# Moving the start addresses of three large SBUF tiles and of the pools after them

## The chip, the core and the metric

The kernel runs on one core of a Trainium2 chip. The metric is the device time of one execution in microseconds, lower is better; the time before is 2186.32 us, the median of three runs (2185.72 to 2187.77). The engines that matter are TensorE (PE in the profile; its weight loads are listed separately as PEld), VectorE (DVE), ScalarE (ACT), GpSimd (POOL) and SyncE (SP), whose queue issues most of the transfers. The on-chip memory (SBUF) has 128 partitions; a tile occupies the same byte range in every partition, and "address" below means the byte offset of a tile's start within a partition.

## What is computed

A two-layer decoder trunk on a sequence of 1024 tokens with 1024 features, all in float32:

```python
for layer in range(DEPTH):              # DEPTH = 2
    if layer < N_A_LAYERS:              # layer 0: HGRN2 gated linear recurrence, 8 heads of 128
        mix = hgrn2_mixer(h, hgrn_w_in[layer], lower_bounds[layer], hgrn_gnorm_w[layer], hgrn_w_out[layer])
    else:                               # layer 1: sliding-window attention, 16 query and 4 key/value heads
        mix = swa_sink_mixer(h, k_shared, v_shared, swa_w_q[j], swa_sinks[j], bias, mask, swa_w_out[j])
    h = layer_norm(ALPHA * h + mix, ln_mix_g[layer], ln_mix_b[layer])
    ff = conv_ffn(h, ffn_w_in[layer], ffn_conv_w[layer], ffn_conv_b[layer], ffn_w_out[layer])
    h = layer_norm(ALPHA * h + ff, ln_ffn_g[layer], ln_ffn_b[layer])

def conv_ffn(h, w_in, conv_w, conv_b, w_out):   # 1024 -> 2 x 2816 -> 1024
    u = causal_depthwise_conv(h @ w_in, conv_w) + conv_b
    a, b = jnp.split(u, 2, axis=-1)
    return (jax.nn.silu(a) * b) @ w_out
```

## The kernel before

**Precision by splitting.** A float32 operand is split into a high part in a reduced float format (`F32R`) and the low rest. `split` (L216) makes the high part with a ScalarE cast (L218) and the low part with a VectorE subtraction (L166). A product is then three matmuls into one PSUM accumulator, made by `mm3` (L190 to L194): high weights by high data (L191), high weights by low data (L192), low weights by high data (L193). Each matmul has a moving operand (the data that stream through the array, 512 or 256 columns of 4 bytes per partition) and a stationary operand (a 128x128 block, 512 bytes per partition), which a weight load puts into the array while the matmul before it runs. In the profile a matmul's name is written `out<-moving,stationary`; where both operands lie in the same tile, only one name stands.

**The large tiles.** All of them live in SBUF:

- `T` holds the transposed activations in both parts, 64 KiB per partition: 2 parts x 8 blocks x 1024 tokens. It is the moving operand of most products and, in token-major products, the stationary one.
- `Y` (32 KiB) is a row buffer: activations, evacuated products, raw weights.
- `HL` (48 KiB) holds weights or activations in two parts, in slots of 8 KiB or pieces of 4 KiB.
- `HT` (12 KiB) belongs to the pool opened for each feed-forward layer and extends `HL`: pieces 12 to 14 of the weights (`weight_load`) and slot 6 of the down projection (`operands`).
- `rx0` to `rx2` (4 KiB each, in the same pool) receive raw weights from DRAM. In the mixers the same addresses hold `raw0` to `raw2`.
- `TX` (48 KiB, class `Up`) holds three derived activation matrices in two parts. In the down projection its place is taken by `R`.

**The stages.** The order on TensorE is: the HGRN2 mixer (0 to 524 us), its output projection with layer norm and transposition (to 590 us), the up projection of the feed-forward (to 925 us), the down projection (to 1140 us), attention (to 1486 us), its output projection (to 1552 us), the second up projection (to 1887 us) and the second down projection (to the end). Both feed-forward matrices are multiplied with a seven-product scheme on 2x2 blocks. In the up projection (class `Up`, `run` and `product`) each of 22 column blocks runs the products in the order 1, 2, 6, 7, 4, 5, 3; each product is four `mm3`, thus 12 matmuls of 512 columns. Products 1, 2, 4 and 5 take their moving operand from `T`, products 6, 7 and 3 from `TX`. Their stationary operands lie in `HL` for odd column blocks, and in `HL` and `HT` for even ones; products 6 and 7 of an even block use `HT`, and so does product 3 of every third block. In the down projection (class `Down`, `operands` and `product`) both operands of a matmul lie in the same slot, in `HL`, `HT` or `T`.

**The order of the work** is written out by hand: nearly everything is issued within manual schedules, and an `Order` object places vector work between matmuls by a table of costs. None of that depends on addresses.

**Where the tiles lie.** A pool hands out addresses in the order in which its tiles are declared, and pools follow each other in the order in which they are opened. The pool `cp` begins at byte 1152. Its first tiles are `T`, `Y` and `HL`, followed by small constants (`ident`, `nhalf`, `par`, `cwt`, `lbt`, `msk`); after it comes the pool `sm` with small statistics, and then the pool of the current stage. The addresses of the built program, in bytes of a partition:

| tile | start | remainder by 512 | remainder by 64 |
|---|---|---|---|
| `T` | 1152 | 128 | 0 |
| `Y` | 66688 | 128 | 0 |
| `HL` | 99456 | 128 | 0 |
| `HT`, `raw0` | 152032 | 480 | 32 |
| `rx0` (`rx1`, `rx2` 4096 and 8192 further) | 164320 | 480 | 32 |
| `TX`, `R` | 176608 | 480 | 32 |
| work tiles of the recurrence (`V`, `G`, `qs`, `kp`, `qp`, `St`, `og` and others) | from 164320 | 480 | 32 |
| attention's `Kh`; `Kl`, `Vt`; `q`, `X` | 164320; 181792, 189984; from 205408 | 480; 32; 96 | 32 |

Of the kernel before, what the change touches and what calls it, by code (L numbers as in the profile page):

```python
# [10 lines left out]
F32 = mybir.dt.float32  # L11
F32R = mybir.dt.float32r
# [4 lines left out]
P = 128  # L17
S = 1024
D = 1024
NB = S // P  # L20
KC = D // P
# [86 lines left out]
def trunk(ctx: ExitStack, tc: tile.TileContext, a: dict, out: bass.AP):  # L108
# [4 lines left out]

    cp = ctx.enter_context(tc.tile_pool(name="cp", bufs=1))
    sm = ctx.enter_context(tc.tile_pool(name="sm", bufs=2))
    mmp = ctx.enter_context(tc.tile_pool(name="mmp", bufs=4, space=PS))
    axp = ctx.enter_context(tc.tile_pool(name="axp", bufs=2, space=PS))
    drp = ctx.enter_context(tc.tile_pool(name="drp", bufs=1, space=bass.MemoryType.DRAM))

    T = cp.tile([P, 2, KC, S], F32R, name="T")  # L120
    Y = cp.tile([P, 8, D], F32, name="Y")
    HL = cp.tile([P, 12, 1024], F32R, name="HL")
    ident = cp.tile([P, P], F32, name="ident")
    nhalf = cp.tile([P, 1], F32, name="nhalf")
    par = cp.tile([P, 17], F32, name="par")
    cwt = cp.tile([P, 2, 4, 2 * NF], F32, name="cwt")
    lbt = cp.tile([P, 2, NH], F32, name="lbt")
    msk = cp.tile([P, 7 * BL + P], U8, name="msk")
    h2d = drp.tile([P, 8, D], F32, name="h2d")
    ynd = drp.tile([P, 8, D], F32, name="ynd")  # L130
    gd = drp.tile([P, NF, S], F32, name="gd")
# [11 lines left out]
    def urgent():  # L143

        return tc.high_priority(offset=300)
# [8 lines left out]
    def hl_at(i):  # L154
        return HL[:, 2 * i:2 * i + 2, :]

# [33 lines left out]
    def mm3(ps, st, mv, start, stop, n=512):  # L190
        nc.tensor.matmul(ps, st(0), mv(0), start=start, stop=False)  # L191
        nc.tensor.matmul(ps, st(0), mv(1), start=False, stop=False)  # L192
        nc.tensor.matmul(ps, st(1), mv(0), start=False, stop=stop)  # L193
        od.t += 3 * n / 2365.0  # L194
# [5 lines left out]
    def tr(ps, src):  # L200
        nc.tensor.transpose(ps, src, ident)  # L201
        od.t += 0.109

    def proj_T(hl, half, ps):
        for kc in range(KC):
            mm3(ps, lambda i: hl[:, i, kc, :], lambda i: T[:, i, kc, half * 512:(half + 1) * 512],
                kc == 0, kc == KC - 1)
            od.tick()

    def proj_tok(us, tp, ps):  # L210
        for i in range(2):
            for kc in range(KC):
                mm3(ps[:, i * 256:(i + 1) * 256], lambda j: T[:, j, kc, (2 * tp + i) * P:(2 * tp + i + 1) * P],
                    lambda j: us[kc // 4][:, j, kc % 4, :], kc == 0, kc == KC - 1, n=256)
                od.tick()

    def split(hi, lo, src, eng=None):
        nc.scalar.copy(hi, src)  # L218
        return low_part(lo, src, hi, eng)
# [8 lines left out]
    def ln_half(tb, i):  # L228

        if tb not in half_stats:  # L230
            half_stats[tb] = sm.tile([P, 2, 6], F32, name="st", bufs=8)
        nc.vector.bn_stats(half_stats[tb][:, i, :], Y[:, tb, i * 512:(i + 1) * 512])

    def ln_stats(tb):
        st = half_stats.pop(tb)
        mv = sm.tile([P, 2], F32, name="mv")
        rs = sm.tile([P, 1], F32, name="rs")
        nc.vector.bn_aggr(mv, st)
        nc.vector.tensor_scalar(rs, mv[:, 1:2], 1.0, LN_EPS, op0=ALU.mult, op1=ALU.add)  # L239
        nc.gpsimd.tensor_tensor(rs, rs, nhalf, op=ALU.pow)  # L240
        return mv, rs

    def ln_affine(tb, rows, dst, n=1):

        y = Y[:, tb, :]
        mv, rs = ln_stats(tb)
# [8 lines left out]
    def turn_block(tb):  # L255

        ps = psax()
        for kc in range(KC):
            tr(ps[:, kc * P:(kc + 1) * P], Y[:, tb, kc * P:(kc + 1) * P])
        ts = slice(tb * P, (tb + 1) * P)  # L260
        split(T[:, 0, :, ts], T[:, 1, :, ts], ps.rearrange("p (k t) -> p k t", k=KC))

# [10 lines left out]
    def Y_to_T(h0, h1, t0, t1, eng=None):  # L273
        ts = slice(t0 * P, t1 * P)
        split(T[:, 0, h0:h1, ts], T[:, 1, h0:h1, ts], Y[:, h0:h1, ts], eng)

# [17 lines left out]
    def out_part(ps, us, tb, kcs, first=0, last=KC - 1):  # L294
        for kc in kcs:
            mm3(ps, lambda j: T[:, j, kc, tb * P:(tb + 1) * P], lambda j: us[kc][:, j, :], kc == first, kc == last)
            od.tick()

    def out_proj(us, begun, rows, resid, ff, ln):
        tasks, late = [], []  # L300
        for tb in range(NB):
            nc.sync.dma_start(Y[:, tb, :], resid(tb))
        for tb, ps in enumerate(begun):
            out_part(ps, us, tb, [KC - 1])
        for dh in range(2):
# [3 lines left out]
            for tb in range(NB):  # L309
# [8 lines left out]
                else:  # L318
                    ps = psmm()
                    out_part(ps, late if dh else us, tb, range(KC))  # L320
                y = Y[:, tb, dh * 512:(dh + 1) * 512]
                with urgent() if dh else nullcontext():
# [18 lines left out]
    def piece(j):  # L341

        t = HL[:, j, :] if j < 12 else tail["R"][:, j - 12, :]
        return t.rearrange("p (h n) -> p h n", h=2)

    class Up:
# [6 lines left out]
        def row_loads(self):  # L353

            l, b = self.l, a["ln_mix_b"]
            self.rows = HL[:, 7, :].bitcast(F32), self.rx[1]
            nc.sync.dma_start(self.rows[0], bass.AP(tensor=gd1.tensor, offset=gd1.offset + l * D, ap=[[0, P], [1, D]]))
            nc.sync.dma_start(self.rows[1], bass.AP(tensor=b.tensor, offset=b.offset + l * D, ap=[[0, P], [1, D]]))

        def ln(self, tb):  # L360
# [6 lines left out]
            with urgent():  # L367
                for q in range(2):
# [4 lines left out]
                    if tb < 4:  # L373
                        split(T[:, 0, ks, ts], T[:, 1, ks, ts], pv)
                        nc.scalar.copy(hf[:, ks], pv)
# [21 lines left out]
        def weight_load(self, fc):  # L397


            whole = lambda j: (HL[:, j, :] if j < 12 else tail["R"][:, j - 12, :])  # L400
            ws = [whole((0 if fc % 2 else 8) + i) for i in range(6)] + [whole((14, 6, 7)[fc % 3])]
# [1077 lines left out]
def build(arrays):  # L1479
    import concourse.bacc as bacc  # L1480

    nc = bacc.Bacc("TRN2", target_bir_lowering=False, num_devices=1, dynamic_dma_scratch_size=1024)
    aps = {n: nc.dram_tensor(f"in_{n}_dram", v.shape, mybir.dt.from_np(v.dtype), kind="ExternalInput").ap()
           for n, v in arrays.items()}
    out = nc.dram_tensor("out_0_dram", (1, S, D), F32, kind="ExternalOutput").ap()
    with tile.TileContext(nc) as tc, tc.manual_schedule(engines={mybir.EngineType.PE}):
        trunk(tc, aps, out)
    return nc
# [10 lines left out]
```

## Time and profile before

| what | value |
|---|---|
| median of three runs | 2186.32 us (2185.72 to 2187.77) |
| span of the profiled execution (first to last instruction) | 2184.9 us |
| difference between that median and that span | 1.4 us |
| TensorE matmuls busy | 2164.9 us, 99% of the span |
| TensorE weight loads busy | 1811.8 us, 83% |
| VectorE busy | 1762.3 us, 81% |
| ScalarE busy | 893.8 us, 41% |
| GpSimd busy | 120.3 us, 6% |
| mean granted TensorE clock | 0.998 |

The profile is one execution on the chip. Its page gives busy times, the clock in 40 slices, the chain of work that ended last and the costliest groups. Three further views of the trace are used: groups of instructions with their shapes kept apart (name, shape, count, union of busy time, mean duration of one in ns, idle time before), windows (in each stretch of time, the busy time of an engine and the number of instructions that it started there), and the timeline (start, duration, engine, line, names). Consecutive matmuls overlap in the array: a 512-column matmul is shown as lasting about 390 ns, while the next one starts about 227 ns after it. The pace of TensorE is therefore the distance from start to start; the mean duration of a group moves with it, but is not it.

### The profile page before, as it was taken

What the parts mean: (1) busy time and instruction counts of PE and PEld (TensorE: products, weight loads), DVE (VectorE), ACT (ScalarE), POOL (GpSimd) and SP (SyncE); (2) the same over time, 40 slices, a digit from 0 to 9 for tenths busy, and PEclk for the clock granted to TensorE, in tenths of its full rate; (3) what the DMA queues carried; (4) which work ended last, traced back from release to release, by engine and by line L of the source; (5) the groups of instructions that cost most, each with busy time, mean ns of one, the idle gap of its engine ahead of it and who ended that gap; (6) DMA issues with size and microseconds to landing.
All of it is one profiled execution on the core that took longest, in us unless ns stands there. A gap on an engine that the chain in (4) does not pass through costs nothing.

```text
span 2184.9 us, 33220 instructions
## 1 busy us (share of the span) xinstructions
PE 2164.9 (99%) x13188; PEld 1811.8 (83%) x13188; DVE 1762.3 (81%) x2388; ACT 893.8 (41%) x1457; POOL 120.3 (6%) x135
## 2 busy tenths in 40 slices
PE   9999999999999999999999999999999999999998
PEld 8888888898878888888888888878888888888887
DVE  3776665667999988888978568969999988878986
ACT  3233333342444444344433256743544444444430
POOL 1000000000100000000001123211000000000001
PEclk9999999999999999999999999999999999999999
DMA  5654533305223222228854411133223222249762
GB/s 197 232 169 161 183 136 101 99 21 175 98 75 106 87 78 81 83 97 263 290 183 155 126 32 28 32 108 115 87 96 96 79 87 77 78 139 325 235 204 94
DMA packets 229844, 279.05 MB, mean 128 GB/s; under 512 B 29960, under 2 KB 158648, under 8 KB 226872
## 3 DMA queue, kind: packets, MB, share of 16 engines
q1 hardware_dynamic: 228736, 276.53, 38.8%
q8 instruction: 104, 1.70, 0.3%
q10 hardware_dynamic: 856, 0.37, 0.1%
q14 instruction: 52, 0.43, 0.1%
q0 software_dynamic: 96, 0.02, 0.0%
HBM read 213.94 MB, written 62.94 MB: 127 GB/s over the span
## 4 chain that ended last, share of the span: by engine, by line
PE 95%; DVE 4%; ACT 1%; issue 1%; DMA 0%; SPq 0%; DVEq 0%; POOL 0%; ACTq 0%; POOLq 0%
PE psmm L191 20%; PE psmm L193 19%; PE psmm L192 19%; PE psax L192 9%; PE psax L193 9%; PE psax L191 9%; PE psax L197 3%; PE psax L201 1%; PE psmm L201 1%; PE psmm L197 1%; PE psax L1290 1%; DVE HL L166 0%; DVE T L166 0%; PE psmm L735 0%; DVE Y L470 0%
## 5 line engine op out<-in xcount | busy, mean ns | idle before, releaser
L191 PE MATMUL psmm<-T,HL 128*128 128x512 f32 x768 | 307.5, 400 | 0.0
L192 PE MATMUL psmm<-T,HL 128*128 128x512 f32 x768 | 300.3, 391 | 0.0
L193 PE MATMUL psmm<-T,HL 128*128 128x512 f32 x768 | 300.2, 391 | 0.0
L470 DVE SCALAR_TENSOR_TENSOR Y<-Y,cwt 128x1023 f32<-128x1023 f32 (+1 forms) x176 | 225.1, 1281 | 42.7 <-ACT Y L468 39.5
L218 ACT CAST HL<-rx 128x1024 fp32r<-128x1024 f32 (+1 forms) x151 | 151.0, 1004 | 199.6 <-PE psmm L192 48.8
L191 PE MATMUL psmm<-HL,T 128*128 128x256 f32 (+1 forms) x656 | 198.4, 302 | 0.0
L193 PE MATMUL psmm<-HL,T 128*128 128x256 f32 (+1 forms) x656 | 194.3, 296 | 1.4 <-DVE T L166 1.4
L192 PE MATMUL psmm<-HL,T 128*128 128x256 f32 (+1 forms) x656 | 194.0, 296 | 0.0
L166 DVE TENSOR_TENSOR HL<-rx,HL 128x1024 fp32r<-128x1024 f32 (+1 forms) x151 | 174.6, 1161 | 13.4 <-ACT HL L218 13.1
L193 PEld LDWEIGHTS psmm<-T,HL 128*128 128x128 f32 x768 | 144.2, 188 | 31.4
L191 PEld LDWEIGHTS psmm<-T,HL 128*128 128x128 f32 x768 | 144.3, 188 | 30.9 <-issue 0.8
L192 PEld LDWEIGHTS psmm<-T,HL 128*128 128x128 f32 x768 | 144.4, 188 | 28.1
L468 ACT ACTIVATE Y<-Y,cwt 128x1024 f32<-128x1024 f32 x88 | 109.0, 1238 | 103.5 <-DVE Y L457 94.4
L192 PE MATMUL psax<-T,HL 128*128 128x512 f32 x352 | 137.7, 391 | 0.0
L191 PE MATMUL psax<-T,HL 128*128 128x512 f32 x352 | 137.7, 391 | 0.0
L193 PE MATMUL psax<-T,HL 128*128 128x512 f32 x352 | 137.4, 390 | 0.0
L191 PEld LDWEIGHTS psmm<-HL,T 128*128 128x128 f32 x656 | 125.2, 191 | 6.6 <-issue 2.9
L193 PEld LDWEIGHTS psmm<-HL,T 128*128 128x128 f32 x656 | 125.2, 191 | 5.2 <-DVE T L166 2.0
L192 PEld LDWEIGHTS psmm<-HL,T 128*128 128x128 f32 x656 | 125.4, 191 | 3.3
L240 POOL TENSOR_TENSOR rs<-rs,nhalf 128x1 f32<-128x1 f32 x32 | 45.6, 1425 | 1415.4 <-DVE rs L239 1415.4
L166 DVE TENSOR_TENSOR HL<-raw,HL 128x1024 fp32r<-128x1024 f32 x51 | 62.4, 1226 | 66.9 <-ACT HL L173 66.6
L218 ACT CAST HT<-rx 128x1024 fp32r<-128x1024 f32 (+1 forms) x37 | 35.5, 959 | 114.3 <-DVE rx L424 75.1
(293 smaller groups left out, 5113.0 us busy)
## 6 DMA issues: line engine op xcount, KB each, us to landing
rx<-in_ffn_w_in_dram SPq DMA_DIRECT2D x136, 256.0 KB, 3.4
rx<-gd SPq DMA_DIRECT2D x118, 256.0 KB, 3.6
Y<-in_ffn_w_out_dram SPq DMA_DIRECT2D x44, 512.0 KB, 5.7
bsd<-Y SPq DMA_DIRECT2D x22, 1024.0 KB, 4.5
gd<-Y SPq DMA_DIRECT2D x44, 512.0 KB, 2.6
rx<-in_ffn_w_out_dram SPq DMA_DIRECT2D x54, 256.0 KB, 3.6
R<-bsd SPq DMA_DIRECT2D x44, 256.0 KB, 4.9
Y<-in_ffn_w_in_dram SPq DMA_DIRECT2D x40, 256.0 KB, 3.3
```

Of the source, the lines that this page charges most:

```text
L166: make = lambda e: e.tensor_tensor(lo, src, hi.bitcast(F32), op=ALU.subtract)
L191: nc.tensor.matmul(ps, st(0), mv(0), start=start, stop=False)
L192: nc.tensor.matmul(ps, st(0), mv(1), start=False, stop=False)
L193: nc.tensor.matmul(ps, st(1), mv(0), start=False, stop=stop)
L197: nc.tensor.matmul(ps, lhsT, rhs, start=start, stop=stop, **kw)
L201: nc.tensor.transpose(ps, src, ident)
L218: nc.scalar.copy(hi, src)
L240: nc.gpsimd.tensor_tensor(rs, rs, nhalf, op=ALU.pow)
L468: nc.scalar.activation(c, u, AF.Identity, bias=cwt[:, l, 3, ci:ci + 1], scale=cwt[:, l, 2, ci:ci + 1])
L470: nc.vector.scalar_tensor_tensor(c[:, sh:], u[:, :S - sh], cwt[:, l, 2 - sh, ci:ci + 1], c[:, sh:], op0=ALU.mult, op1=ALU.add)
L1290: nc.tensor.matmul(pv[:, e, jj, lo:], q[bp // 2][es, e, qs], Kl[es, pp, ks] if low else Kh[:, pp, e, ks], start=not low and jj == 0, stop= ...
```

## The change

Small tiles are declared first in the pool `cp`, followed by a new 480-byte tile `edge`, and only then `T`, `Y` and `HL`. A new pool `sp`, opened after `sm`, holds a 64-byte tile `rim`. No instruction reads or writes `edge` or `rim`.

```diff
     sm = ctx.enter_context(tc.tile_pool(name="sm", bufs=2))
+    sp = ctx.enter_context(tc.tile_pool(name="sp", bufs=1))
...
-    T = cp.tile([P, 2, KC, S], F32R, name="T")
-    Y = cp.tile([P, 8, D], F32, name="Y")
-    HL = cp.tile([P, 12, 1024], F32R, name="HL")
     ident = cp.tile([P, P], F32, name="ident")
     nhalf = cp.tile([P, 1], F32, name="nhalf")
     par = cp.tile([P, 17], F32, name="par")
     cwt = cp.tile([P, 2, 4, 2 * NF], F32, name="cwt")
     lbt = cp.tile([P, 2, NH], F32, name="lbt")
     msk = cp.tile([P, 7 * BL + P], U8, name="msk")
+    edge = cp.tile([P, 120], F32, name="edge")
+    T = cp.tile([P, 2, KC, S], F32R, name="T")
+    Y = cp.tile([P, 8, D], F32, name="Y")
+    HL = cp.tile([P, 12, 1024], F32R, name="HL")
+    rim = sp.tile([P, 16], F32, name="rim")
```

Every engine's instructions stand in the same order with the same waits as before; only addresses differ. In the built program:

| tile | start before | start after | moved by | remainder by 512 before, after |
|---|---|---|---|---|
| `ident` | 148608 | 1152 | -147456 | 128, 128 |
| `T` | 1152 | 4096 | 2944 | 128, 0 |
| `Y` | 66688 | 69632 | 2944 | 128, 0 |
| `HL` | 99456 | 102400 | 2944 | 128, 0 |
| `HT`, `raw0` | 152032 | 152576 | 544 | 480, 0 |
| `rx0` | 164320 | 164864 | 544 | 480, 0 |
| `TX`, `R` | 176608 | 177152 | 544 | 480, 0 |
| work tiles of the recurrence | from 164320 | from 164864 | 544 | 480, 0 |
| attention's `Kh`; `Kl`, `Vt`; `q`, `X` | 164320; 181792, 189984; from 205408 | each 544 further | 544 | 480, 0; 32, 64; 96, 128 |

`T`, `Y` and `HL` keep their distances from each other, and so do the later tiles among themselves; the distance between the two sets shrinks by 2400 bytes.

## Prediction

> **What bounds the kernel now.** I read the page first, its busy line and its chain.
>
> ```profile
> span 2184.9 us, 33220 instructions
> ...
> PE 2164.9 (99%) x13188; PEld 1811.8 (83%) x13188; DVE 1762.3 (81%) x2388; ACT 893.8 (41%) x1457; POOL 120.3 (6%) x135
> ...
> PE 95%; DVE 4%; ACT 1%; issue 1%; DMA 0%; SPq 0%; DVEq 0%; POOL 0%; ACTq 0%; POOLq 0%
> ```
>
> TensorE is busy 99% of the span and makes 95% of the chain of waits, so only what changes its pace, or makes it stop, can move the time. The windows, cut at the stages, show where that pace can be counted (length, PE busy, instructions started, clock, DMA share, GB/s):
>
> ```profile
> 590.00:925.00 335.00, 334.25 (x1455) 1.00 0.27 87
> 925.00:1140.00 215.00, 215.00 (x941) 1.00 0.62 204
> 1552.00:1887.00 335.00, 334.25 (x1454) 1.00 0.27 87
> 1887.00:2172.00 285.00, 285.00 (x1249) 1.00 0.58 193
> 526.00:590.00 64.00, 64.00 (x311) 1.00 0.27 99
> ...
> 0.00:524.00 524.00, 519.02 (x5326) 1.00 0.45 149
> 1140.00:1486.00 346.00, 340.23 (x2114) 1.00 0.30 86
> ```
>
> The first four rows are the two up and the two down projections: 512-column matmuls alone, never idle for longer than 0.75 us in all, at the full clock. Their pace is not uniform: 335 us through 1455 is 230 ns each. The timeline, one product of twelve matmuls after the other, shows which are slow (start, duration, names; moving operand first):
>
> ```profile
> 717.97 0.39 PE L191 MATMUL psmm<-T,HL 128*128 128x512 f32 x1
> ...
> 720.68 0.40 PE L191 MATMUL psmm<-TX,HL 128*128 128x512 f32 x1
> ...
> 722.80 0.39 PE L191 MATMUL psmm<-TX,HL 128*128 128x512 f32 x1
> ...
> 723.50 0.39 PE L191 MATMUL psax<-TX,HL 128*128 128x512 f32 x1
> ...
> 726.30 0.40 PE L191 MATMUL psax<-T,HL 128*128 128x512 f32 x1
> ...
> 729.06 0.39 PE L191 MATMUL psmm<-T,HL 128*128 128x512 f32 x1
> ...
> 731.78 0.40 PE L191 MATMUL psmm<-TX,HL 128*128 128x512 f32 x1
> ```
>
> Each shown start (722.80 apart) opens a product. `T` by `HL` takes 2.71 us (717.97 to 720.68), `TX` by `HL` 2.82 and 2.80, the `T` by `HL` product after it 2.76, the next 2.72 again. That is 226 to 227 ns per matmul in the good case, 233 to 235 with `TX`, and a remainder of slowness that the following product carries off. The last three of a `TX` by `HL` product still take 0.70 us (722.80 to 723.50), 233 ns each: it does not settle. `TX` by `HT` does, after a slow beginning:
>
> ```profile
> 704.22 0.39 PE L191 MATMUL psax<-TX,HT 128*128 128x512 f32 x1
> ...
> 705.35 0.39 PE L193 MATMUL psax<-TX,HT 128*128 128x512 f32 x1
> ```
>
> Five matmuls in 1.13 us, 226 ns. So the tile `TX` is not slow by itself. By the addresses above, `T` and `HL` start 0 past a multiple of 64 bytes, `TX` and `HT` 32 past one. Pairs with the same remainder run at 226 ns, pairs with different ones at 233. That is my reading: the moving stream and the weight load beside it cost more when they are out of step by 32 bytes.
>
> The groups by form carry it over the whole run (count | busy, mean ns of one; each group has its like for the other two lines):
>
> ```profile
> L192 PE MATMUL psmm<-T,HL 128*128 128x512 f32 x768 | 300.3, 391 | 0.0
> L192 PE MATMUL psax<-T,HL 128*128 128x512 f32 x352 | 137.7, 391 | 0.0
> L193 PE MATMUL psmm<-TX,HL 128*128 128x512 f32 x160 | 63.7, 398 | 1.5 <-DVE HL L166 1.5
> L192 PE MATMUL psmm<-TX,HL 128*128 128x512 f32 x160 | 63.4, 396 | 0.0
> L191 PE MATMUL psmm<-TX,HL 128*128 128x512 f32 x160 | 63.1, 394 | 0.0
> L192 PE MATMUL psmm<-T 128*128 128x512 f32 x160 | 62.3, 389 | 0.0
> L192 PE MATMUL psax<-TX,HL 128*128 128x512 f32 x128 | 50.7, 396 | 0.0
> L192 PE MATMUL psmm<-TX,T 128*128 128x512 f32 x128 | 50.6, 396 | 0.0
> L192 PE MATMUL psmm<-TX,HT 128*128 128x512 f32 x128 | 50.2, 392 | 0.0
> L192 PE MATMUL psmm<-HT 128*128 128x512 f32 x28 | 11.0, 394 | 0.0
> ```
>
> `T` alone is the floor, 389 ns. The two groups with unequal remainders, `TX` by `HL` and `TX` by `T`, stand 7 ns above it, as the starts did.
>
> **The change part by part.** It adds no instruction, removes none, moves none and adds no wait: two tiles that nobody touches, and other addresses. After it `T`, `Y`, `HL`, `HT`, `TX`, `R` and the `rx` tiles all start at a multiple of 512, so every pair in the feed-forward has equal remainders.
>
> (1) Up and down projections. At 226.7 ns (2.72 us through 12) the 1455 matmuls of the first window need 329.85 us against 334.25 busy: 4.40 to gain. In the same way 4.63 for the second up, 1.68 for the first down (941) and 1.85 for the second down (1249): 12.56 us. This takes the carried remainders with it, since no product would then leave any. Bounds: nothing below; above, the same sum at 225.8 ns (2.71 through 12), 0.9 ns less on 5099 matmuls, 4.6 more. I take 12.6, because twelve-matmul products at that pace stand beside the slow ones throughout.
>
> (2) Output projections. Products of `TX` by `T` run there between transposes:
>
> ```profile
> L191 PE MATMUL psmm<-TX,T 128*128 128x512 f32 x64 | 25.7, 401 | 0.0
> L193 PE MATMUL psmm<-TX,T 128*128 128x512 f32 x64 | 25.5, 398 | 0.0
> L192 PE MATMUL psmm<-TX,T 128*128 128x512 f32 x64 | 25.2, 394 | 0.0
> ...
> 526.00:590.00 64.00, 64.00 (x311) 52.70 (x310) 62.43 (x99) 22.63 (x38) 11.81 (x8) 1.00 0.27 99
> ```
>
> Above 389 that is 64 x (12 + 9 + 5) = 1.66 us in a stage, part of it the wait after a transpose, and VectorE (third busy number, 62.43) leaves 1.57 us of room. I take half, 0.8 us a stage and 1.6 for both; bounds 0 and 3.1.
>
> (3) Mixers. Their projections already pair `T` with `HL`. The recurrence's and attention's own tiles move together from 32 to 0 past 64 among themselves, so little changes. The nearest rows are the transposes of `X` (remainder 32) and `Y` (0) against `ident`:
>
> ```profile
> L201 PE MATMUL psmm<-ident,X 128*128 128x128 f32 x128 | 21.2, 290 | 2.1 <-DVE T L166 1.5 <-DVE X L1321 0.4
> L201 PE MATMUL psmm<-ident,Y 128*128 128x128 f32 x128 | 16.6, 272 | 0.0
> ```
>
> 18 ns on 128 bounds the gain by 2.3 us, but the first includes waits. A loss is bounded by giving these 128 the excess of `HT` by `HT` over `T`, 5 ns, 0.6 us. I take 0.
>
> (4) VectorE, ScalarE and transfers. Their operands move too. VectorE's rows with all operands at 32 (`HT` from `rx`, `HT`), mixed (`HL` from `rx`, `HL`) and at 0 (`Y` from `Y`) are alike:
>
> ```profile
> L166 DVE TENSOR_TENSOR HL<-rx,HL 128x1024 fp32r<-128x1024 f32 x135 | 164.3, 1218 | 12.8 <-ACT HL L218 12.6 <-DMA rx<-in_ffn_w_out_dram 0.2
> L475 DVE TENSOR_TENSOR Y<-Y 128x1024 f32<-128x1024 f32 x44 | 53.8, 1223 | 1.0
> L166 DVE TENSOR_TENSOR HT<-rx,HT 128x1024 fp32r<-128x1024 f32 x29 | 35.4, 1219 | 2.1 <-ACT HT L218 2.1
> ```
>
> So 0, and TensorE's work covers all of it; its chain share for DMA is 0%. What a faster TensorE meets next is VectorE, 62.43 of 64 us in the output projection: there the cover is thin, which is why I halved (2). For waits of this kind in the rest, and slow entries after a stop, I take off 1 us (bounds 0 and 3).
>
> Sum: 12.6 + 1.6 - 1.0 = 13.2 us. The profiled span becomes 2184.9 - 13.2 = 2171.7; the median stood 1.4 above that span, so 2173 us.
>
> [...]
>
> **The rivals.**
>
> *Nothing moves: 2186.* The start address does not matter, and the slowness belongs to where the `TX` products stand in the order or to how far up in the partition the tile lies. For it: remainder and height go together, as `TX` and `HT` are the upper tiles. Against it: `TX` by `HT`, both high up, settles at 226. [...]
>
> *Half of it: 2181.* Pairs at a multiple of 512 still clash when both reads begin at the same place, so the `TX` groups come down only to the pace of the slow `T` by `HL` product, 2.76 us or 230 ns, and the carry stays. Then 864 `TX` by `HL` matmuls (160 + 128, three lines each) gain some 4 ns, 3.5 us, and 384 `TX` by `T` the same, 1.5: 5 us. For it: in those slow products `T` and `HL` begin at equal addresses modulo 4096. Against it: the carry dies within the product, which an address clash would not.
>
> *Slower: 2200.* A common start at a multiple of 512 costs by itself: reads and the writes of VectorE and ScalarE all begin in the same place of a 512-byte period, and every `T` by `HL` matmul takes the excess of `HT` by `HT`, equal remainders and yet 394 against 389. On 3360 of them (768 + 352, three lines) that is 5 ns, 16.8 us, while `TX` gains perhaps 3: 2186 + 14. It decides from 4 ns on (3360 x 4 = 13.4). For it: `HT` by `HT` is slow. Against it: those products are short visits among tiles of the other remainder, and begin slow like `TX` by `HT`.
>
> *More: 2160.* `T` and `HL` at 128 past 512 pay something too, which a multiple of 512 removes: half the excess of `HT` by `HT`, 2.5 ns on 5099, would add 12.7 us to the gain. Nothing in the trace shows such a start.
>
> **How the numbers follow.** Forecast 0.62, half 0.15, nothing 0.11, slower 0.08, more 0.04. The likeliest gives 2173. Its own bounds: gains of 9.6 ((2) and (4) at their worst) to 18 (the faster pace), 2168 to 2177. The range must take in the half case and stops short of no change: 2167 to 2183, which leaves out the nothing, slower and more cases, about 2 in 10. A measurement of this kernel tells 0.2%, 4.4 us, from no change. Faster by that: 0.62 + 0.04 and nearly all of the half case, 0.80. Within it: nothing and a rest of the half, 0.11. Slower: 0.09.
>
> **What would show it.** Right: `TX` by `HL`, by `T` and by `HT` at 389 to 391 ns in the groups by form; up windows of about 330 us; the `T` by `HL` product after `TX` in 2.72 us; `T` alone still at 389. Wrong: `TX` groups at 394 to 398 (nothing), at 392 with `T` by `HL` at 391 (half), `T` by `HL` or `T` alone at 393 or more (slower), or a new idle time before TensorE's L191 rows with VectorE as releaser.

## The result and the profile after

The changed kernel takes 2170.54 us (median of 5 runs, 2169.4 to 2172.1) against 2187.16 us for the kernel before, run beside it (median of 5, 2185.72 to 2188.72): ratio 0.9923, 95% interval 0.9911 to 0.9935. Its profiled span is 2170.3 us at a mean granted clock of 0.998, 14.6 us under the span of before; the profiled execution was the slowest of the five (2172.1 us, against 2169.4 to 2170.62 at a clock of 0.999), so the two spans lie closer together than the two medians, which are 16.6 us apart.

The page of after, its span, its busy line and its chain:

```profile
span 2170.3 us, 33220 instructions
...
PE 2149.8 (99%) x13188; PEld 1812.2 (83%) x13188; DVE 1760.9 (81%) x2388; ACT 895.0 (41%) x1457; POOL 119.8 (6%) x135
...
PE 85%; DVE 9%; DMA 3%; issue 2%; ACT 1%; SPq 0%; POOL 0%; DVEq 0%; ACTq 0%; POOLq 0%
```

The same matmuls, 13188, keep TensorE busy for 15.1 us less. Weight loads, VectorE and ScalarE kept their busy times within 1.4 us. TensorE's share of the chain fell from 95% to 85%, and VectorE and a few transfers appear in it. That belongs to this execution and not to the change: in a second profile of the same kernel (e10 below) TensorE has 94%.

The windows of after over the two up and the two down projections (length, TensorE busy, matmuls started, clock, DMA share, GB/s):

```profile
590.00:925.00 335.00, 334.19 (x1475) 1.00 0.27 87
925.00:1140.00 215.00, 214.53 (x947) 1.00 0.63 212
1552.00:1882.00 330.00, 329.19 (x1453) 1.00 0.28 88
1882.00:2157.00 275.00, 274.84 (x1213) 1.00 0.58 198
```

The first window has the same borders as before: 1475 matmuls start where 1455 did, at the same clock. 334.19 through 1475 is 226.6 ns each (229.7 before), and the third and fourth give the same.

The timeline of after, where before showed good and bad products next to each other (start, duration, names; each row shown opens a product of twelve):

```profile
717.71 0.39 PE L194 MATMUL psmm<-TX,HL 128*128 128x512 f32 x1
...
720.43 0.39 PE L194 MATMUL psax<-TX,HL 128*128 128x512 f32 x1
...
723.15 0.39 PE L194 MATMUL psax<-T,HL 128*128 128x512 f32 x1
...
725.87 0.39 PE L194 MATMUL psmm<-T,HL 128*128 128x512 f32 x1
...
728.59 0.39 PE L194 MATMUL psmm<-TX,HL 128*128 128x512 f32 x1
```

Four products, from `TX` and from `T`, take 2.72 us each. The excess of `TX` and the remainder that the next product carried off are both gone. The groups by form of after say it for the whole run (count | busy, mean ns | idle before):

```profile
L195 PE MATMUL psmm<-T,HL 128*128 128x512 f32 x768 | 299.6, 390 | 0.0
...
L196 PE MATMUL psmm<-TX,HL 128*128 128x512 f32 x160 | 62.5, 390 | 1.6 <-DVE HL L169 1.6
L195 PE MATMUL psmm<-TX,HL 128*128 128x512 f32 x160 | 62.3, 389 | 0.0
...
L195 PE MATMUL psmm<-T 128*128 128x512 f32 x160 | 62.2, 389 | 0.0
...
L195 PE MATMUL psmm<-TX,T 128*128 128x512 f32 x128 | 49.9, 390 | 0.0
...
L195 PE MATMUL psmm<-TX,HT 128*128 128x512 f32 x128 | 49.8, 389 | 0.0
...
L195 PE MATMUL psmm<-HT 128*128 128x512 f32 x28 | 10.9, 389 | 0.0
```

On the lines shown all pairs stand at the floor of 389 to 390 ns. (On the first of the three lines `T` by `HL` stays at 400 ns, and `TX` by `T` goes from 402 to 397.) `HT` by `HT`, 394 before although both starts were equal, came down too.

Where the time came from, as distances between the starts of the same matmuls in both traces, cut near the borders of the stages (times counted from the first matmul, 2.79 us into the span of before):

| stage | before, us | after, us | difference |
|---|---|---|---|
| first mixer | 524.04 | 523.78 | -0.26 |
| first output projection | 65.97 | 64.91 | -1.05 |
| first up projection | 334.99 | 330.23 | -4.77 |
| first down projection | 215.16 | 214.07 | -1.09 |
| attention mixer | 345.99 | 346.37 | +0.38 |
| second output projection | 66.06 | 64.72 | -1.34 |
| second up projection | 335.01 | 330.23 | -4.78 |
| second down projection | 284.96 | 283.35 | -1.61 |

### The profile page after: what moved, and what is told of

The parts are those of the page before. It is cut to its first block, busy times and chain, and to the rows that moved or that the text cites. A ratio compares the mean times of both kernels' runs of the same rounds, so it can differ in the third digit from the quotient of the medians.

```text
span 2170.3 us, 33220 instructions
## 1 busy us (share of the span) xinstructions
PE 2149.8 (99%) x13188; PEld 1812.2 (83%) x13188; DVE 1760.9 (81%) x2388; ACT 895.0 (41%) x1457; POOL 119.8 (6%) x135
## 4 chain that ended last, share of the span: by engine, by line
PE 85%; DVE 9%; DMA 3%; issue 2%; ACT 1%; SPq 0%; POOL 0%; DVEq 0%; ACTq 0%; POOLq 0%
PE psmm L194 18%; PE psmm L196 17%; PE psmm L195 17%; PE psax L194 8%; PE psax L196 8%; PE psax L195 8%; PE psax L200 3%; PE psax L204 1%; DVE T L169 1%; PE psmm L204 1%; DVE Y L473 1%; PE psmm L200 1%; PE psax L1293 1%; DVE HL L169 1%; DMA R<-bsd 0%
## 5 line engine op out<-in xcount | busy, mean ns | idle before, releaser
L169 DVE TENSOR_TENSOR HL<-rx,HL 128x1024 fp32r<-128x1024 f32 (+1 forms) x151 | 174.4, 1160 | 14.2 <-ACT HL L221 13.9
```

The costliest lines, as they stand in the source:

```text
L169: make = lambda e: e.tensor_tensor(lo, src, hi.bitcast(F32), op=ALU.subtract)
```

## The experiments

Two sets of tiles matter: the early one (`T`, `Y`, `HL` in `cp`) and the later ones (`HT`, `rx`, `TX`, `R` in the stage's pools). Fillers shift each by whole steps of 32 bytes, so starts can be set without touching an instruction. The outcome first, for finding one's way; "distance" is that between the starts of the two sets modulo 256, and the column of `TX` by `HL` is the mean duration of its group on the second of the three lines.

| kernel | early set, start mod 512 | later set, start mod 512 | distance mod 256 | median, us | ratio to before | `TX` by `HL`, ns |
|---|---|---|---|---|---|---|
| before | 128 | 480 | 96 | 2187 | 1 | 396 |
| after | 0 | 0 | 0 | 2170.54 | 0.9923 | 389 |
| e1 | 0 | 480 | 224 | 2184.47 | 0.9984 | 395 |
| e2 | 128 | 0 | 128 | 2180.44 | 0.9968 | 394 |
| e3 | 32 | 32 | 0 | 2172.56 | 0.9932 | 389 |
| e4 | 0 | 448 | 192 | 2183.47 | 0.9979 | 394 |
| e5 | 128 | `TX` 128, `HT` 480 | `TX` 0, `HT` 96 | 2178.31 | 0.9959 | 389 |
| e6 | 128 | 128 | 0 | 2172.53 | 0.9929 | 389 |
| e8 | 0 | 256 | 0 | 2172.30 | 0.9928 | 389 |

### Which part of the change does it: e1 and e4

The changed kernel with the second filler half as long:

```diff
-    rim = sp.tile([P, 16], F32, name="rim")
+    rim = sp.tile([P, 8], F32, name="rim")
```

> The changed kernel with the second filler cut from 64 to 32 bytes: T, Y and HL stay at multiples of 4096, HT, rx, TX and the work tiles go back to 32 past a multiple of 64. Pair theory (a matmul is slow when the remainders by 64 of its moving operand and of the weights loaded beside it differ): TX by HL and TX by T back at 394 to 398 ns, time 2186, as before. Theory of the large tiles (their multiple of 4096 brought the gain): 2171.

And without it:

```diff
-    sp = ctx.enter_context(tc.tile_pool(name="sp", bufs=1))
...
-    rim = sp.tile([P, 16], F32, name="rim")
```

> The changed kernel without the second filler: T, Y and HL at multiples of 4096, the later pools 448 past a multiple of 512, which is 0 by 64. Pair theory by 64: 2171 and 389 ns, so that the second filler is not needed with the first. If the period is 128, 256 or 512 bytes: TX by HL at 394 to 398 and 2186.

Measured: e1 2184.47 us against 2187.45, ratio 0.9984 (0.9975 to 0.9993), e4 2183.47, ratio 0.9979 (0.9970 to 0.9988). In both, `T`, `Y` and `HL` begin at a multiple of 4096 exactly as after, and about a fifth (e1) or a quarter (e4) of the gain is left. The groups by form of e1, and then of e4:

```profile
L195 PE MATMUL psmm<-TX,HL 128*128 128x512 f32 x160 | 63.3, 395 | 0.0
```

```profile
L193 PE MATMUL psmm<-TX,HL 128*128 128x512 f32 x160 | 63.1, 394 | 0.0
```

The 64 bytes of `rim` are needed. Aligning the large tiles alone is not what pays. In e4 the later set begins at 448, a multiple of 64, as the early set does: equal remainders by 64, and `TX` by `HL` is slow all the same.

### The modulus: e2, e8 and the pair of starts: e3, e6

The kernel before with one filler behind the small statistics, of 32 bytes in e2 (the later set goes to 0) and of 160 bytes in e6 (all go to 128):

```diff
+    sp = ctx.enter_context(tc.tile_pool(name="sp", bufs=1))
...
+    rim = sp.tile([P, 8], F32, name="rim")
```

> The kernel before with one 32-byte filler behind the pool of small statistics and nothing else: T, Y and HL stay at 128 past a multiple of 512, the later pools go to a multiple of 512. Pair theory by 64: all of the gain, 2171, every 512-column group at 389 ns. If the remainders have to agree by 512, or if the large tiles matter: 2186 or in between, TX by HL above 391.

```diff
+    sp = ctx.enter_context(tc.tile_pool(name="sp", bufs=1))
...
+    rim = sp.tile([P, 40], F32, name="rim")
```

> The kernel before with one filler of 160 bytes behind the pool of small statistics: all feed-forward tiles, ident and the recurrence's tiles at 128 past a multiple of 512, none at a multiple of 512. Pair theory by 512: every 512-column feed-forward group at 389, 2171, as the changed kernel; perhaps 0.5 us less, because ident stays in step with T and Y. Theory that the starts have to be multiples of 512: 2180 to 2187.

The changed kernel with `rim` at 320 bytes, so that the later set lies at 256:

```diff
-    rim = sp.tile([P, 16], F32, name="rim")
+    rim = sp.tile([P, 80], F32, name="rim")
```

> The changed kernel with the second filler at 320 bytes: T, Y and HL at a multiple of 512, the later pools 256 past one. Period of 256: 2171 and TX by HL at 389. Period of 512: TX by HL and TX by T at 394 to 396, 2181 to 2185, as at 64 and 128.

The changed kernel with `edge` 32 bytes longer, so that all large tiles lie at 32 past a multiple of 512:

```diff
-    edge = cp.tile([P, 120], F32, name="edge")
+    edge = cp.tile([P, 128], F32, name="edge")
```

> The changed kernel with the first filler grown from 480 to 512 bytes: T, Y, HL and all later pools start 32 past a multiple of 512, so that all remainders agree and none is 0. Pair theory: 2171, TX by HL and TX by HT at 389. Theory of absolute starts (a read that begins off a multiple of 64 costs, whatever the other one does): every 512-column group at 394 or more; 5099 matmuls of the up and down projections at 5 ns more are 25 us, 2196.

Measured: e2 2180.44 us, ratio 0.9968 (0.9956 to 0.9980); e6 2172.53 against 2187.32, ratio 0.9929 (0.9917 to 0.9941); e8 2172.30, ratio 0.9928 (0.9915 to 0.9942); e3 2172.56, ratio 0.9932 (0.9920 to 0.9945). The groups by form of e2:

```profile
L194 PE MATMUL psmm<-TX,HL 128*128 128x512 f32 x160 | 63.1, 394 | 0.0
...
L194 PE MATMUL psmm<-TX,HT 128*128 128x512 f32 x128 | 49.8, 389 | 0.0
```

`TX` and `HT` lie at 0 and run at the floor; `TX` with `HL`, 128 bytes out, does not. With that the reading by 64, which gave 2171 us for e2 and for e4, has failed in both. Of e8, e6 and e3:

```profile
L195 PE MATMUL psmm<-TX,HL 128*128 128x512 f32 x160 | 62.3, 389 | 0.0
```

```profile
L194 PE MATMUL psmm<-TX,HL 128*128 128x512 f32 x160 | 62.3, 389 | 0.0
```

```profile
L195 PE MATMUL psmm<-TX,HL 128*128 128x512 f32 x160 | 62.2, 389 | 0.0
```

A distance of 256 is as good as none (e8); 128, 192 and 224 are not (e2, e4, e1). So the period that fits every start tried is 256 bytes. The place of the pair as a whole does not count: 0, 32 and 128 past a multiple of 512 give the same 389 ns. And one filler of 160 bytes in the kernel before (e6) brings what the change brings with its new order and two fillers, as far as the intervals can tell: e3, e6 and e8 lie 1.8 to 2.0 us above after, within them.

### The tile or the pair: e5

The kernel before with a gap that moves `TX` and `R` alone to 128, in the feed-forward's pool after the `rx` tiles:

```diff
             tail["raw"] = [pool.tile([P, 1024], F32, name=f"rx{i}") for i in range(3)]
+            pool.tile([P, 40], F32, name="gap")
```

> The kernel before with a 160-byte filler ahead of TX (and R) alone: TX at 128 past a multiple of 512, as T and HL are; HT stays at 480. Pair theory by 512: TX by HL and TX by T drop from 394-398 to 389, TX by HT, in step before and out of step now, rises from 390-393 to 394-396, and HT by HT stays slow; TX by HL and by T save about 9.5 us, 720 TX by HT lose about 3: 2180. Theory that each tile by itself has to lie well, or that TX is slow for its height in the partition: TX by HT falls with the others or nothing changes, 2175 or 2187.

Measured: 2178.31 us, ratio 0.9959 (0.9946 to 0.9971). The groups by form of e5:

```profile
L192 PE MATMUL psmm<-TX,HL 128*128 128x512 f32 x160 | 62.3, 389 | 0.0
...
L192 PE MATMUL psmm<-TX,HT 128*128 128x512 f32 x128 | 50.6, 396 | 0.0
...
L192 PE MATMUL psmm<-HT 128*128 128x512 f32 x28 | 11.0, 394 | 0.0
```

The same tile `TX`, at one address, is at the floor with `HL` and 7 ns above it with `HT`, which stayed at 480. Before, it was the other way round: 396 with `HL`, 392 with `HT`. It is the pair that counts, not the tile and not how high in the partition it lies.

### Making it worse: e9

If distance alone decides, moving `HL` off must slow down the largest group of all, which before and after run at the floor. The changed kernel with `HL` at 128 and the rest at 0:

```diff
+    gap = cp.tile([P, 32], F32, name="gap")
     HL = cp.tile([P, 12, 1024], F32R, name="HL")
-    rim = sp.tile([P, 16], F32, name="rim")
+    rim = sp.tile([P, 112], F32, name="rim")
```

> The changed kernel with 128 bytes between Y and HL (and the second filler grown so that the later pools stay at a multiple of 512): HL alone is 128 past a multiple of 256, out of step with T, TX and HT. Pair theory by 256, doubling the suspected cost: T by HL, HL by T and TX by HL of 512 columns, 3360 + 384 + 864, at 394 to 396 instead of 389, 4608 x 6 to 7 ns = 28 to 32 us, TX by T and TX by HT at 389; 2199 to 2203, and up to 12 us more if the 1728 matmuls of 256 columns pay as much each. Theory that TX or the upper part of the partition is what costs: 2171.

Measured: 2194.98 us against 2187.02, ratio 1.0033 (1.0022 to 1.0044), span 2191.0 us, 20.7 above that of after. The first up window of e9, and its groups by form:

```profile
590.00:925.00 335.00, 334.33 (x1444) 1.00 0.27 85
```

```profile
L196 PE MATMUL psmm<-T,HL 128*128 128x512 f32 x768 | 302.7, 394 | 0.0
...
L196 PE MATMUL psmm<-HL,T 128*128 128x256 f32 x576 | 162.0, 281 | 0.0
...
L196 PE MATMUL psmm<-TX,HL 128*128 128x512 f32 x160 | 63.1, 395 | 0.0
...
L196 PE MATMUL psmm<-TX,T 128*128 128x512 f32 x128 | 49.9, 390 | 0.0
...
L196 PE MATMUL psmm<-TX,HT 128*128 128x512 f32 x128 | 49.9, 390 | 0.0
```

The cause works in both directions. `T` by `HL` and `TX` by `HL` at 512 columns are slow now, the pairs without `HL` stay at the floor, `HL` with itself does too (389 ns on the second line), and the pace of the window is 231.5 ns (334.33 through 1444). The size fell short of what I expected, 2199 to 2203 us: an excess of 4 to 6 ns instead of 6 to 7, and the 256-column products pay nothing, 281 ns against 283 in the same group of after:

```profile
L195 PE MATMUL psmm<-HL,T 128*128 128x256 f32 x576 | 162.8, 283 | 0.0
```

### A better version: e7, e10, e11, e12

e7 is e6 with two gaps in attention's pool, which bring `Kh`, `Kl`, `Vt`, `q` and `X` to 128 too:

```diff
+        at.tile([P, 112], F32, name="gap1")
...
+        at.tile([P, 112], F32, name="gap2")
```

> The kernel of the one filler, with 448 bytes added behind each of attention's two 64-byte tiles, so that Kh, Kl, Vt, W0, q and X also lie at 128 past a multiple of 512. Pair theory: attention's stage, 346.0 us before, loses up to the 1.6 us that its TensorE groups stand above the pace, 2169.5 to 2171. If the attention stage is set by its waits: 2171, as the one filler.

It took 2170.65 us, ratio 0.9926 (0.9913 to 0.9938), and its attention stage 344.29 us against 346.37 of after. But e6 has 344.59 there without the gaps, and e5, whose attention tiles lie where those of before lie, 344.46. So the three were run again side by side, unchanged: after (e10), e6 (e11), e7 (e12).

> The changed kernel itself, beside the two below on one chip: 2170 to 2172, ratio 0.992 to 0.993.

> The kernel before with the one filler of 160 bytes, again: if keeping ident in step with T and Y is worth the 0.5 us, at or just below the changed kernel, 2170 to 2171.5; otherwise no difference that can be told.

> The same with attention's tiles in step as well, again: 2169 to 2171 if attention's stage gains 1.5 us by it, otherwise as the one filler.

2170.99, 2171.92 and 2170.86 us, ratios 0.9924 (0.9911 to 0.9938), 0.9929 (0.9916 to 0.9943) and 0.9924 (0.9910 to 0.9938). Attention took 346.35, 346.20 and 345.80 us. The 2 us of e7 did not come back. The granted clock accounts for them. Here are the same 3.4 us of attention, first of e6 and then of e11, which are the same kernel (length, TensorE busy, matmuls started, clock, DMA share, GB/s):

```profile
1442.88:1446.29 3.41, 3.41 (x17) 1.00 0.80 293
```

```profile
1442.88:1446.29 3.41, 3.41 (x11) 0.50 0.82 274
```

At half the clock 3.4 us lose 1.7 us by estimate, and the stage differs by 1.61 (346.20 against 344.59). The profiles of before, after, e10, e11 and e12 have such a fall of the clock in attention (0.51 from 1449.40 to 1452.80 us of before and from 1442.60 to 1446.00 us of after; the mean granted clock of all five is 0.998), those of e5, e6 and e7 have none (mean 0.999). Like compared with like, the stage is 0.3 us shorter with the gaps (e7 against e6) and 0.4 us (e12 against e11). Why the clock falls in some executions these runs don't show. No version beats the changed kernel, and the one-filler version is level with it.

## Why the prediction was right

**The bound.** TensorE's pace was what set the time, and it is what changed. The views that showed the slow pace before, windows and timeline, show 226.6 ns throughout after.

**The mechanism, and its wrong step.** "The moving stream and the weight load beside it cost more when they are out of step" held as far as the pair goes: e5 and e9 switch the cost off and on by single tiles (`TX` by `HL` 389 ns in e5, 395 in e9). That it is the load beside the stream, rather than the weights already in use, was argued and stays so. "Pairs with the same remainder" by 64 did not. e2 (128 apart) and e4 (192 apart) have equal remainders by 64 and are slow (`TX` by `HL` 394 ns in both); the period that fits the runs is 256. In the feed-forward, where I read it, the only distances before were 0 and 96, which cannot tell 64 from 256, and I took the finer one. So the step that failed is the period. The forecast stood all the same because the change goes to multiples of 512, which satisfies both; that was luck. For a change with the early set at 0 and the later one at 448, the same reasoning would have given some 2173, and e4 took 2183.47.

**(1) Up and down projections.** Predicted 4.40, 4.63, 1.68 and 1.85; the stages gave 4.77, 4.78, 1.09 and 1.61. The pace of 226.7 ns was right (226.6). The first down projection fell 0.6 short. In the waits of after, TensorE's own, there is one in that stage, and none in that of before (total us, times, longest):

```profile
PE psax L194 <- DVE Y L594: 0.5, 1, 0.5
```

and the chain of waits of after goes there through transfers (start, us, what):

```profile
1001.09 4.55 DMA rx<-in_ffn_w_out_dram
...
1013.57 5.57 DMA rx<-in_ffn_w_out_dram
```

So half a microsecond was handed to a wait for VectorE, itself fed late by weights from memory. In e10, the stage gained 1.86, so the wait is not always met.

**(2) Output projections.** 0.8 each predicted, 1.05 and 1.34 measured. I had halved the sum for fear of VectorE. The window of after, all engines (busy and count of TensorE, its loads, VectorE, ScalarE and GpSimd, then clock, DMA share, GB/s):

```profile
526.00:590.00 64.00, 64.00 (x316) 53.52 (x315) 63.45 (x102) 24.21 (x39) 11.20 (x8) 1.00 0.27 99
```

VectorE rose from 62.43 to 63.45 of 64 us and TensorE still did not stop: 316 matmuls instead of 311. The room was as thin as read, and in this execution it was enough. In e6 and e12, with the same pairs in step, the first output projection gained only 0.5 and 0.6, with one wait of 0.2 us for ScalarE there; so the halved term is not wrong for every execution.

**(3) Mixers.** 0 predicted; -0.26 and +0.38 measured, within what the repeats scatter. The bounding rows stayed, in the groups by form of after:

```profile
L204 PE MATMUL psmm<-ident,X 128*128 128x128 f32 x128 | 21.3, 290 | 2.1 <-DVE T L169 1.5 <-DVE X L1324 0.4
...
L204 PE MATMUL psmm<-ident,Y 128*128 128x128 f32 x128 | 16.7, 272 | 0.0
```

**(4) The other engines.** VectorE's rows did not move, as read before: `HL` from `rx` 1217 ns (1218), `Y` from `Y` 1222 (1223), `HT` 1219 (1219). Of the 1 us taken off for new waits, 0.6 appeared, in the first down projection.

The stages sum to 14.5 us and the span to 14.6, instead of 13.2. The mis-sized terms: the ups 0.5 more, the output projections 0.8 more, the downs 0.8 less, the mixers 0.1 less, on 14.2 before the deduction of 1.0, whose place the shortfall of the downs took. The other half of the miss, from 2173 to 2170.54, is the step from span to median: 0.2 this time instead of 1.4, because the profiled execution was the slowest of the five. The runs take 1.7 to 1.9 us more than their own spans, so neither 0.2 nor 1.4 is a property of one execution.

**The rivals.** *Nothing moves* fell by the result, and its ground with e5: there `TX` moved by 160 bytes and nothing in the order, and `TX` by `HL` reached the floor. At 512 columns the traces show a difference by the start of the tiles alone, 389 against 394 to 398 ns for `TX` by `HL`. Whether it is the weight load beside the running matmul that costs it is not shown. *Half of it* fell with all groups at 389 and the 2.72 us product after a `TX` product. *Slower*: `HT` by `HT`, on which it rested, runs at 389 at a multiple of 512, and also with all tiles at 32 (e3) or at 128 (e6), and stays at 394 in e5, at 480 among tiles out of step. That its neighbours made it slow fits this; all tiles at 480 was not tried. *More*: e6 leaves all large tiles at 128 and is level with after, so no cost of 128 shows.

## What to carry to other kernels

When TensorE is the bound and every matmul loads weights, compare the start-to-start distance of products that differ only in their tiles; here about 3% between them, 226 to 227 ns against 233 to 235, lay in the addresses, which the code doesn't show. Let tiles that meet in a matmul of 512 columns begin at the same place modulo 256 bytes of a partition, which took 16.6 us off this kernel's 2187.16, by a filler behind the small tiles where needed; which place it is made no difference here (389 ns at 0, 32 and 128). Check a modulus with distances that tell it from its divisors, before a forecast rests on it.

## What the runs showed of the hardware

A matmul of 512 columns with a weight load for each went at 226.6 ns when moving tile and weights started at the same place modulo 256 bytes, and at 231 to 235 ns when not; distances of 96, 128, 192 and 224 were slow, 0 and 256 fast. The distances are those of the tiles' starts; inside the tiles of the up projection the blocks lie whole multiples of 512 bytes further. Steps finer than 32 bytes were not tried. Products of 256 columns paid nothing: `HL` by `T` took 281 ns in e9, 128 bytes out of step, and 283 in after, in step.

How much a wrong distance cost differed: the whole kernel took 2187 us at 96, 2184.47 at 224, 2183.47 at 192 and 2180.44 at 128.

The slowness outlasted its cause. In the timeline of e1 two products of `TX` by `HT`, in step, follow one of `T` by `HL`, also in step, but the two sets lie 224 apart:

```profile
703.00 0.39 PE L194 MATMUL psax<-TX,HT 128*128 128x512 f32 x1
...
704.39 0.39 PE L194 MATMUL psax<-TX,HT 128*128 128x512 f32 x1
...
708.01 0.39 PE L195 MATMUL psax<-TX,HT 128*128 128x512 f32 x1
```

The first six matmuls take 1.39 us, 232 ns each, the next sixteen 3.62 us, 226 ns each. So a change from one place to another was paid for too, in products that are in step themselves; that fits `HT` by `HT` before.

This payment goes with the order of the whole times. Worked out from the starts in the first up projection, `TX` by `HL` runs at 233 to 234 ns from its seventh matmul on at all four distances, but the first six `TX` by `HT` matmuls behind a `T` by `HL` product take 232.6 ns each at a distance of 96, 230.7 at 224, 228.8 at 192 and 227.4 at 128 (226.7 at 0). Why the distances come in this order is open.

The mechanism behind it is not settled. In every product that is out of step the weights of a matmul and those loaded beside it are of the same tile, but for its last matmul, so the runs can't say which of the two must be in step with the moving stream.
